# Embeddings behind each gate, rows through DRAM, norm weights inside the split, and squares summed on VectorE

## The chip, the cores and the metric

The kernel runs on one core of one Trainium2 chip. A core has five engines with a queue of instructions each: TensorE (PE; its weight loads are listed as PEld), VectorE (DVE), ScalarE (ACT), GpSimd (POOL) and SyncE (SP), which here only issues DMAs. TensorE writes its results into PSUM, eight banks of 128 partitions x 512 fp32 numbers; the other data lie in SBUF. An engine works through its queue in order, and waits on semaphores for what other engines or DMAs owe it.

The metric is the device time of one execution in microseconds (us), lower is better. Three timed executions of the kernel before gave 1090.06, 1090.41 and 1091.36; the median is 1090.41 us.

## The reference

Two layers over 256 tokens of width 2048, all in fp32, batch 1. Cut to what matters here:

```python
for i in range(2):
    hn = rmsnorm(h, e_norm[0] if i == 0 else o_norm[0])
    if i == 0:
        u = hn @ e_w_in[0]                    # q, f, i, z_a, x_b, z_b, 1024 wide each
        ya = head_rmsnorm(hgrn2(q, f, i, lbs[0]), a_norm[0]) * silu(z_a)
        yb = rg_lru(causal_conv(x_b, ...), ...) * silu(z_b)
        mix = concatenate([ya, yb]) @ e_w_out[0]
    else:
        u = hn @ o_w_in[0]                    # qk, v, og, z: 2048 each; 8 + 8 gate columns
        yc = mlstm(q, k, v, li, lf)           # running maximum of the gates as stabiliser
        yc = head_rmsnorm(yc, c_norm[0]) * sigmoid(og) * silu(z)
        mix = yc @ o_w_out[0]
    h = h + mix
    pl = rmsnorm(p[i] @ ple_w[i], ple_norm[i])      # the embedding, 256 -> 2048
    h = h + sigmoid(h @ ple_gate_w[i]) * pl
return rmsnorm(h, final_norm)
```

`rmsnorm(x, g)` is `x * rsqrt(mean(x*x) + 1e-6) * g`, along the 2048 features of a token.

## The kernel before

**Products.** Every large product is done in split precision: an fp32 operand becomes a rounded part `hi` (type fp32r) and a rest `lo = x - hi`, and hi·hi, hi·lo and lo·hi are added up in PSUM. `load_weights` (L111) has SP load 128x1024 pieces into `raw` (five buffers), ScalarE cast them into `whi` (L122) and VectorE subtract into `wlo` (L123), four buffers each. Activations are split in the same way into `ahl` tiles (`act_pair`, `split_act`; L137, L138): hi and lo side by side, 256 tokens each.

There are two forms of product. `block` (L146) has features on the partitions: 16 matmuls of 128x512 (L153, the weights' hi against hi and lo of the activations), then 16 of 128x256 (L159, the weights' lo), into one bank `mm`. `project_tok` (L179) has tokens on the partitions: two banks `mm`, one for each half of the tokens, four quarters of the inner dimension, three matmuls for each step (L194 to L196). `gate_tok` (L450) follows it with a tanh on ScalarE (L454) and a product on VectorE (L455).

**Banks.** `mm` (pool `pm`) has three PSUM banks, `mx` (pool `px`) three, `st` (pool `pst`) two.

**Side work.** What is not a large product runs beside them, as generators in named lanes (`start`, L63). `pump` (L74), called once in each `block` and once in each quarter of `project_tok`, lets each lane go on to its next `yield`; its instructions are queued behind the last large matmul, cast and split. `drain` (L81) runs a lane to its end. The order of the instructions on an engine is otherwise set by a planner with estimated costs; casts and splits of weights are put forward (`high_priority`).

**Norms.** The norm weight is applied to the activations before they are split (`gained`, L273: two scalings on VectorE, L277, then `split_act`); the factor of the token is applied behind the product. `add_square` (L265) squares on ScalarE and adds on the engine that it is given: POOL for x in the first layer (L406; VectorE for the last two of eight), for the embeddings and for h. `folded` adds the halves on POOL. `rs_tok` (L216) sums over the partitions with small matmuls (L221) and takes the inverse root on VectorE: a column `rt`, one number per token on its partition. Where a row over the tokens is needed on every partition (`rs`), `free_copy` (L259) makes it with `to_free` (L228): a diagonal matrix `dg` on VectorE and an fp32 matmul with ones (L234), copied by ScalarE. Three calls: the two layers' norms (`finish_norm`, L415; tile `hrs`), the first layer's embedding (`ple_norm`, L322; tile `plrs`).

**Layer 0.** i projection for two halves (`i_proj`, L629; the first one loads x as it goes), f and q, then the lanes `att` (HGRN2, two head groups; read out at L638) and `rg` (RG-LRU) beside the projections of x_b and the gates z_a, z_b. `out_proj` (L345) with `eo`, then the gate of the embedding (`ple_gate`, L357).

**Layer 1.** v, the gate columns, q and k, then og and z by `gate_tok`. The lane `mix` holds `gate_stats` (L829) and for each of four pairs of heads `mix(j)` (L865). `gate_stats` ends in `Mx`, the running maximum, 8 heads x 256 tokens; `split8` splits it and `spread` (L246) puts the rows of two heads on all partitions of an `mx` bank by four matmuls (L250, L251); `wt` is the constant minus these rows (L872, L873).

Behind the z gates come the features: `feature_major` (L427, lane `fm`) transposes a gate's output `u` (L438) and splits it with the norm weight into `y` (L446 on ScalarE, L447 on VectorE). The second embedding is `embed(g)` (L956), four parts of twelve matmuls (L964 to L966) into two `mm` banks, copied by VectorE (L968), squared by ScalarE (L970). The loop at L974 to L988 runs gate 0, gate 1, embed 0, gate 2, embed 1, gate 3, embed 2, a pump, embed 3, and drains `fm`. Then the rows of `ple_norm[1]` are loaded by POOL and multiplied into the parts on POOL (L993), the second row `fnr` is loaded, the sums of squares `pss` become `rp` (L999 to L1004), and `out_proj` runs with `oo` on `y`.

## Time and profile before

| | us |
|---|---|
| median of three timed executions | 1090.41 |
| the profiled execution | 1090.81 |
| its span, first to last instruction | 1089.0 |

DMA moves 200.31 MB, 184 GB/s over the span; SyncE's queue takes 53.0% of the 16 DMA engines' time, GpSimd's 1.2%.

How the lines are read. A line of the waits, "PE mm L194 <- DVE u L455: 1.9, 3, 1.2", says that TensorE's instructions of line 194, which write `mm`, stood for `u` of VectorE's line 455: 1.9 us in all, three times, 1.2 the longest. A line of the chain has the start in us, the length in us, and what ran; "x16" merges sixteen instructions. A line of the timeline has start and length in us, engine, line, operation, the tiles written and read and their shapes; in brackets stands the idle time before it and what ended it. A line of groups has "xcount | busy us in all, mean ns of one | idle us before". Matmuls overlap: a wide one is listed with 0.39 us but starts 0.23 after the one before. A line of windows has the stretch, then for PE, PEld, DVE, ACT and POOL the busy us and, in brackets, the instructions, then the granted clock, the share of DMA and GB/s.

### The profile page before, as it was taken

The page shows a single profiled execution, that of the slowest core. Times are in us where ns is not written, and L with a number is a line of the kernel's source. Part 1 is how long each engine was busy: PE and PEld are TensorE (multiplying, and loading weights), DVE is VectorE, ACT ScalarE, POOL GpSimd, SP SyncE. Part 2 cuts the span into 40 slices and gives each one's busy share as a digit, 9 for nine tenths or more (in the row PEclk, how much of TensorE's full clock was granted, in tenths as well). Part 3 has the DMA queues.
Part 4 walks back from the last instruction along what each step waited for, and adds up shares of the span by engine and source line. Part 5 has one row for each costly group of instructions (what it writes and reads, how often), then busy time and mean ns, then how long its engine had stood idle before and what let it go on. Part 6 is the DMA issues. An engine that isn't in the chain of part 4 may idle for free.

```text
span 1089.0 us, 16844 instructions
## 1 busy us (share of the span) xinstructions
PE 1064.6 (98%) x6522; PEld 913.0 (84%) x6522; DVE 753.4 (69%) x1121; ACT 580.8 (53%) x850; POOL 86.5 (8%) x74
## 2 busy tenths in 40 slices
PE   7999999999999999999999999999999999999996
PEld 6788888887888888888888888888888878888886
DVE  7968978877767556877544877764456686655565
ACT  6565455688654435555444656644445554434543
POOL 2142200000000000112000000000000120000111
PEclk9999999999999999999999999999999999999998
DMA  8655544446755555555554544445555665555552
GB/s 322 204 193 193 176 161 140 148 136 194 236 198 186 192 192 192 187 186 184 190 193 166 180 156 157 163 168 194 196 190 199 217 202 177 183 189 175 192 174 78
DMA packets 55952, 200.31 MB, mean 184 GB/s; under 512 B 6208, under 2 KB 6592, under 8 KB 55872
## 3 DMA queue, kind: packets, MB, share of 16 engines
q1 hardware_dynamic: 54720, 195.04, 53.0%
q0 software_dynamic: 1152, 4.19, 1.2%
q8 instruction: 51, 0.84, 0.3%
q14 instruction: 29, 0.24, 0.1%
HBM read 197.11 MB, written 2.10 MB: 183 GB/s over the span
## 4 chain that ended last, share of the span: by engine, by line
PE 89%; DVE 5%; ACT 4%; issue 1%; DMA 1%; SPq 0%; DVEq 0%; ACTq 0%
PE mm L153 31%; PE mm L159 17%; PE mm L194 12%; PE mm L196 12%; PE mm L195 12%; DVE wlo L123 2%; ACT whi L122 1%; PE mm L1058 1%; PE mm L1056 1%; PE mm L1057 1%; DMA raw<-in_pw_dram 1%; PE nu L897 1%; PE mx L556 1%; DVE ahl L138 0%; ACT L695 0%
## 5 line engine op out<-in xcount | busy, mean ns | idle before, releaser
L123 DVE TENSOR_TENSOR wlo<-raw,whi 128x1024 fp32r<-128x1024 f32 (+1 forms) x361 | 450.7, 1273 | 244.8 <-ACT whi L122 136.1
L122 ACT CAST whi<-raw 128x1024 fp32r<-128x1024 f32 (+1 forms) x361 | 377.1, 1047 | 331.8 <-PE mm L153 171.8
L153 PE MATMUL mm<-ahl,whi 128*128 128x512 f32 x1536 | 367.7, 392 | 2.7 <-DVE ahl L447 1.9
L153 PEld LDWEIGHTS mm<-ahl,whi 128*128 128x128 f32 x1536 | 282.3, 188 | 59.1 <-DVE ahl L447 3.0
L194 PE MATMUL mm<-whi,ahl 128*128 128x512 f32 x608 | 239.8, 394 | 2.4 <-DVE u L455 1.9
L196 PE MATMUL mm<-whi,ahl 128*128 128x512 f32 x608 | 237.1, 390 | 1.8 <-DVE ahl L138 1.8
L195 PE MATMUL mm<-wlo,ahl 128*128 128x512 f32 x608 | 237.2, 390 | 0.8 <-DVE wlo L123 0.8
L159 PE MATMUL mm<-ahl,wlo 128*128 128x256 f32 x1536 | 202.4, 285 | 0.0
L159 PEld LDWEIGHTS mm<-ahl,wlo 128*128 128x128 f32 x1536 | 195.4, 191 | 6.2
L194 PEld LDWEIGHTS mm<-whi,ahl 128*128 128x128 f32 x608 | 114.3, 188 | 27.6 <-DVE u L455 3.1
L196 PEld LDWEIGHTS mm<-whi,ahl 128*128 128x128 f32 x608 | 114.2, 188 | 27.0 <-DVE ahl L138 3.1
L195 PEld LDWEIGHTS mm<-wlo,ahl 128*128 128x128 f32 x608 | 114.3, 188 | 23.9 <-DVE wlo L123 1.1
L165 ACT COPY sm<-mm 128x256 f32<-128x256 f32 x64 | 23.7, 371 | 45.0 <-PE mm L159 45.0
L271 POOL TENSOR_TENSOR acc<-acc,sq 128x512 f32<-128x512 f32 x11 | 19.9, 1812 | 212.6 <-ACT sq L270 212.4
L166 DVE TENSOR_TENSOR mg<-mm,sm 128x256 f32<-128x256 f32 x64 | 26.7, 418 | 0.0
L782 DVE SCALAR_TENSOR_TENSOR qk<-mg,prm,qk 128x255 f32<-128x255 f32 (+2 forms) x48 | 21.3, 479 | 6.8 <-ACT qk L779 6.5
L949 POOL DMA_DIRECT2D row<-in_rows_dram x4 | 2.2, 553 | 279.8 <-DVE u L981 268.1
L1044 POOL TENSOR_TENSOR pl<-pl,row 128x512 f32<-128x512 f32 x6 | 9.2, 1533 | 153.7 <-ACT sq L1028 153.7
L446 ACT ACTIVATE ahl<-mx,prm 128x256 fp32r<-128x256 f32 x24 | 10.9, 473 | 14.6 <-PE mx L438 8.3
L1056 PE MATMUL mm<-whi,ahl 128*128 128x256 f32 x64 | 18.3, 286 | 0.0
L138 DVE TENSOR_TENSOR ahl<-hq,ahl 128x512 fp32r<-128x512 f32 x16 | 10.7, 690 | 10.8 <-ACT ahl L137 10.8
L1057 PE MATMUL mm<-wlo,ahl 128*128 128x256 f32 x64 | 18.1, 283 | 0.0
(299 smaller groups left out, 822.8 us busy)
## 6 DMA issues: line engine op xcount, KB each, us to landing
raw<-in_ew_dram SPq DMA_DIRECT2D x64, 512.0 KB, 4.8
raw<-in_g_dram SPq DMA_DIRECT2D x56, 512.0 KB, 4.3
raw<-in_eo_dram SPq DMA_DIRECT2D x32, 512.0 KB, 4.6
raw<-in_ov_dram SPq DMA_DIRECT2D x32, 512.0 KB, 4.1
raw<-in_oqk_dram SPq DMA_DIRECT2D x32, 512.0 KB, 4.5
raw<-in_oog_dram SPq DMA_DIRECT2D x32, 512.0 KB, 4.2
raw<-in_oz_dram SPq DMA_DIRECT2D x32, 512.0 KB, 4.1
raw<-in_oo_dram SPq DMA_DIRECT2D x32, 512.0 KB, 4.6
```

The source lines that it names most:

```text
L122: last["act"] = s.copy(h, r).ins
L123: last["dve"] = v.tensor_tensor(out=l, in0=r, in1=h.bitcast(F32), op=ALU.subtract).ins
L153: last["pe"] = te.matmul(ps, parts[k // 8][0][:, c:c + P], act[k // 2][2][:, (k % 2) * 512:(k % 2 + 1) * 512], start=(k == 0), stop=False).ins
L159: last["pe"] = te.matmul(ps[:, T:2 * T], parts[k // 8][1][:, c:c + P], act[k // 2][0][:, k % 2], start=False, stop=(k == KT - 1)).ins
L165: s.copy(small, ps[:, T:2 * T])
L166: v.tensor_tensor(out=dst, in0=ps[:, 0:T], in1=small, op=ALU.add)
L194: te.matmul(ps[hf], xh, wh, start=(k == 0), stop=False)
L195: te.matmul(ps[hf], xh, wl, start=False, stop=False)
L196: last["pe"] = te.matmul(ps[hf], xl, wh, start=False, stop=(k == KT - 1)).ins
L782: v.scalar_tensor_tensor(dst[:, sh:T], pi[:, 0:T - sh], pc("ccw", k * 16 + b), dst[:, sh:T], op0=ALU.mult, op1=ALU.add)
L1056: te.matmul(ps[hf], xh, wh, start=(k == 0), stop=False)
L1057: te.matmul(ps[hf], xh, wl, start=False, stop=False)
```

## The change

- `to_free`, `split8`, the old `spread` and the constant `identr` go. `free_copy` writes the column `rt` (256 single numbers) to a DRAM tile with a DMA of POOL, and reads it back on all partitions with a second one.
- `Mx` is written to DRAM by POOL in `gate_stats`. `spread(j)` is now a DMA of POOL that reads two heads' rows on all partitions into an SBUF tile `spr` (two buffers); those of pairs 0 and 1 are issued at the start of `mix(0)`, which gets one more `yield`, those of 2 and 3 from `mix(0)` and `mix(1)`.
- `gained` has ScalarE scale and cast in one instruction and VectorE multiply and subtract in one, two halves each; the tile between goes.
- All squares of x are added on VectorE.
- In the attention, the third product (`Ac`) takes an `st` bank; the product of the read out (L660) goes from POOL to VectorE; the `memset` of A comes later.
- `embed(j)` runs behind gate j, on `st` banks; it loads its part of the row of `ple_norm[1]` with POOL and multiplies it in where it copied before. POOL's products (L993) go.
- Behind the last embedding three pumps are run. The first block of `out_proj` with `oo` takes its matmuls in the order hi of 12 steps, then what is left of `fm`, lo of the 12, hi of the last 4, lo of the last 4. The sums `pss` and the load of `fnr` go into a lane `en` beside the blocks that follow.

```diff
@@ -54,6 +54,7 @@
     pm = ctx.enter_context(tc.tile_pool(name="pm", bufs=3, space=PSUM))
     pst = ctx.enter_context(tc.tile_pool(name="pst", bufs=2, space=PSUM))
+    dr = ctx.enter_context(tc.tile_pool(name="dr", bufs=2, space=bass.MemoryType.DRAM))
 
 
 
@@ -143,21 +144,34 @@
         te.matmul(o, whi, x[1][:, k], start=False, stop=False)
         last["pe"] = te.matmul(o, wlo, x[0][:, k], start=False, stop=end).ins
 
-    def block(w, act):
-
+    def block(w, act, mid=None):
 
         ps = pm.tile([P, 512], F32, name="mm", tag="mm")
         parts = load_weights(w)
-        for k in range(KT):
-            c = (k % 8) * P
-            last["pe"] = te.matmul(ps, parts[k // 8][0][:, c:c + P],
-                                   act[k // 2][2][:, (k % 2) * 512:(k % 2 + 1) * 512],
-                                   start=(k == 0), stop=False).ins
-        pump()
-        for k in range(KT):
-            c = (k % 8) * P
-            last["pe"] = te.matmul(ps[:, T:2 * T], parts[k // 8][1][:, c:c + P], act[k // 2][0][:, k % 2],
-                                   start=False, stop=(k == KT - 1)).ins
+
+        def his(ks):
+            for k in ks:
+                c = (k % 8) * P
+                last["pe"] = te.matmul(ps, parts[k // 8][0][:, c:c + P],
+                                       act[k // 2][2][:, (k % 2) * 512:(k % 2 + 1) * 512],
+                                       start=(k == 0), stop=False).ins
+
+        def los(ks):
+            for k in ks:
+                c = (k % 8) * P
+                last["pe"] = te.matmul(ps[:, T:2 * T], parts[k // 8][1][:, c:c + P], act[k // 2][0][:, k % 2],
+                                       start=False, stop=(k == KT - 1)).ins
+
+        if mid is None:
+            his(range(KT))
+            pump()
+            los(range(KT))
+        else:
+            his(range(12))
+            mid()
+            los(range(12))
+            his(range(12, KT))
+            los(range(12, KT))
         return ps
 
     def merge(dst, ps):
@@ -225,31 +239,6 @@
             v.tensor_scalar(y[:, hf:hf + 1], st[hf][:, 0:1], 1.0 / D, EPS, op0=ALU.mult, op1=ALU.add)
         return rsqrt_cols(y)
 
-    def to_free(rt):
...
-    def split8(x, name):
...
-    def spread(o, parts, h):
...
     def folded(acc, *more):
         gp.tensor_tensor(out=acc[:, 0:T], in0=acc[:, 0:T], in1=acc[:, T:2 * T], op=ALU.add)
         for x in more:
@@ -257,9 +246,10 @@
         return acc[:, 0:T]
 
     def free_copy(rt, name):
-        ps = to_free(rt)
+        d = dr.tile([T], F32, name=name + "d", tag="rsd")
+        gp.dma_start(out=d.rearrange("(h p) -> p h", h=2), in_=rt)
         rs = tp.tile([P, T], F32, name=name, tag="rsb")
-        s.copy(rs, ps)
+        gp.dma_start(out=rs, in_=d.partition_broadcast(P))
         return rs
 
     def add_square(eng, acc, src, first):
@@ -271,11 +261,12 @@
             eng.tensor_tensor(out=acc, in0=acc, in1=sq, op=ALU.add)
 
     def gained(src, g, j):
-        n = tp.tile([P, 512], F32, name="hn", tag="hn", bufs=3)
+        hi, lo, both = act_pair()
         for i in range(2):
-            k = 2 * j + i
-            v.tensor_scalar(n[:, i * T:(i + 1) * T], src[:, i * T:(i + 1) * T], pc(g, k), None, op0=ALU.mult)
-        return split_act(n, "g")
+            w, x = pc(g, 2 * j + i), src[:, i * T:(i + 1) * T]
+            s.activation(hi[:, i], x, AF.Copy, scale=w)
+            v.scalar_tensor_tensor(lo[:, i], x, w, hi[:, i].bitcast(F32), op0=ALU.mult, op1=ALU.subtract)
+        return hi, lo, both
 
     def gate_split(w, pair, act, rs, src, single):
         hi, lo, both = act_pair()
@@ -342,12 +333,12 @@
             if j % 2:
                 yield
 
-    def out_proj(hq, w, y):
+    def out_proj(hq, w, y, mid=None):
 
         act = []
         for j in range(8):
             for i in range(2):
-                ps = block(w[2 * j + i], y)
+                ps = block(w[2 * j + i], y, mid if i == j == 0 else None)
                 hh = pair_of(hq, j)[:, i * T:(i + 1) * T]
                 v.tensor_tensor(out=hh, in0=ps[:, 0:T], in1=hh, op=ALU.add)
                 v.tensor_tensor(out=hh, in0=ps[:, T:2 * T], in1=hh, op=ALU.add)
...
@@ -403,7 +393,7 @@
         xq.append(t)
         for j in (2 * i, 2 * i + 1):
             acth.append(gained(pair_of(xq, j), "en", j))
-            add_square(gp if j < 6 else v, acc, pair_of(xq, j), j == 0)
+            add_square(v, acc, pair_of(xq, j), j == 0)
         if i == 3:
             start("norm", finish_norm([folded(acc)], 0))
 
...
@@ -531,7 +520,6 @@
         res = {}
 
         A = m0.tile([P, 8, P], F32, name="A", tag="A", bufs=1)
-        gp.memset(A, 0.0)
 
         def attention(g):
 
@@ -540,6 +528,8 @@
             C = m0.tile([P, 8, 32], F32, name="C", tag="C", bufs=1)
             qf = m0.tile([P, 1024], F32, name="qf", tag="qf", bufs=1)
             v.tensor_tensor(out=qf, in0=q, in1=f, op=ALU.mult)
+            if g == 0:
+                gp.memset(A, 0.0)
             yield
             tot = f
             for B in LEVELS:
@@ -614,7 +604,7 @@
                                           (1, k4[:, c, 1], 3, q64[:, c]), (0, k64[:, c], 3, q64[:, c])):
                         te.matmul(p3[32 * x:32 * x + 32, i, 32 * y_:32 * y_ + 32], kk, qq, start=True, stop=True)
                 banks.append(p3)
-            ps = px.tile([P, 512], F32, name="mx", tag="mx")
+            ps = pst.tile([P, 512], F32, name="st", tag="st")
             for c in range(4):
                 cc = slice(c * P, (c + 1) * P)
                 te.matmul(ps[:, cc], kx[:, cc], qx[:, cc], start=True, stop=True)
@@ -657,7 +647,7 @@
                 rc = r[:, hf * 4:(hf + 1) * 4]
                 v.tensor_scalar(rc, rc, norm["rth"][:, hf:hf + 1], None, op0=ALU.mult)
             o8 = o.rearrange("p h (c e) -> p (h c) e", c=4)
-            gp.tensor_tensor(out=o8, in0=o8, in1=r.unsqueeze(2).to_broadcast([P, 8, P]), op=ALU.mult)
+            v.tensor_tensor(out=o8, in0=o8, in1=r.unsqueeze(2).to_broadcast([P, 8, P]), op=ALU.mult)
             res["o", g] = o
 
         def xb_proj(r):
@@ -844,7 +834,9 @@
             v.tensor_tensor_scan(Mx, ones[0:8, :], av, 0.0, op0=ALU.mult, op1=ALU.max)
             v.tensor_tensor(out=enm, in0=Bc, in1=Mx, op=ALU.add)
             s.activation(enm, enm, AF.Exp, scale=-1.0)
-            pM.append(split8(Mx, "Mx"))
+            d = dr.tile([8, T], F32, name="Mxd", tag="Mxd")
+            gp.dma_start(out=d, in_=Mx)
+            pM.append(d)
             yield
             yield
             yield
@@ -862,12 +854,20 @@
 
         den, ss, fac = (m1.tile([P, 16], F32, name=n, bufs=1) for n in ("den", "ss", "fac"))
 
+        spr = {}
+
+        def spread(j):
+            t = m1.tile([P, 2, T], F32, name="spr", tag="spr", bufs=2)
+            gp.dma_start(out=t, in_=pM[0][2 * j:2 * j + 2].partition_broadcast(P))
+            spr[j] = t
+
         def mix(j):
 
-            ps = px.tile([P, 512], F32, name="mx", tag="mx")
-            for i in range(2):
-                spread(ps[:, i * T:(i + 1) * T], pM[0], 2 * j + i)
-            p3 = ps.rearrange("p (i t) -> p i t", i=2)
+            if j == 0:
+                spread(0)
+                spread(1)
+                yield
+            p3 = spr[j]
             wt = m1.tile([P, 2, 384], F32, name="wt", tag="wt", bufs=1)
             v.tensor_tensor(out=wt[:, :, 0:T], in0=tri2.unsqueeze(1).to_broadcast([P, 2, T]), in1=p3, op=ALU.subtract)
             v.tensor_tensor(out=wt[:, :, T:384], in0=tri2[:, 0:P].unsqueeze(1).to_broadcast([P, 2, P]),
@@ -876,6 +876,8 @@
                 hd = 2 * j + i
                 s.activation(wt[:, i, 0:T], wt[:, i, 0:T], AF.Exp, bias=aT[:, hd:hd + 1])
                 s.activation(wt[:, i, T:384], wt[:, i, T:384], AF.Exp, bias=aT[:, 8 + hd:9 + hd])
+            if j < 2:
+                spread(j + 2)
             yield
             yield
             scw = m1.tile([P, 2, 384], F32, name="scw", tag="scw", bufs=2)
@@ -954,10 +956,12 @@
         pss = m1.tile([P, 4, 2], F32, name="pss", bufs=1)
 
         def embed(g):
+            pnr = m1.tile([P, 512], F32, name="pnr", tag="spr", bufs=2)
+            gp.dma_start(out=pnr, in_=a["rows"][0, g * 512:(g + 1) * 512].partition_broadcast(P))
             hi, lo = load_weights(a["pw1"][g // 2], halves=(g % 2,))[0]
             halves = []
             for hf in range(2):
-                ps = pm.tile([P, 512], F32, name="mm", tag="mm")
+                ps = pst.tile([P, 512], F32, name="st", tag="st")
                 for k in range(2):
                     xh, xl = (x[:, k, hf * P:(hf + 1) * P] for x in pact[0:2])
                     wh, wl = (x[:, k * 512:(k + 1) * 512] for x in (hi, lo))
@@ -965,7 +969,7 @@
                     te.matmul(ps, xh, wl, start=False, stop=False)
                     last["pe"] = te.matmul(ps, xl, wh, start=False, stop=(k == 1)).ins
                 pl = m1.tile([P, 512], F32, name="pl", tag="qk", bufs=8)
-                v.tensor_copy(pl, ps)
+                v.tensor_tensor(out=pl, in0=ps, in1=pnr, op=ALU.mult)
                 sq = tp.tile([P, 512], F32, name="sq", tag="sq")
                 s.activation(sq, ps, AF.Square, accum_out=pss[:, g, hf:hf + 1])
                 halves.append(pl)
@@ -981,17 +985,11 @@
                     v.scalar_tensor_tensor(u[:, hf, e], u[:, hf, e], fac[:, c:c + 1], nums[j][:, hf, e],
                                            op0=ALU.mult, op1=ALU.mult)
             start("fm", feature_major(u, "cn", 4 * j, y))
-            if j in (1, 2):
-                embed(j - 1)
-        embed(2)
+            embed(j)
         pump()
-        embed(3)
-        drain("fm")
-        pnr = row(0)
-        for g in range(4):
-            for pl in pls[g]:
-                gp.tensor_tensor(out=pl, in0=pl, in1=pnr[g // 2][:, (g % 2) * 512:(g % 2 + 1) * 512], op=ALU.mult)
-        fnr = row(1)
+        pump()
+        pump()
+        rows = []
 
         def total(x, n):
 
@@ -1001,9 +999,18 @@
             return x[:, 0]
 
         rp = m1.tile([P, 2], F32, name="rp", bufs=1)
-        v.tensor_scalar(rp, rsqrt_cols(total(pss, 4)), 0.5, None, op0=ALU.mult)
-
-        act = out_proj(hq, a["oo"], y)
+
+        def embed_norm():
+            yield
+            yield
+            rows.extend(row(1))
+            v.tensor_scalar(rp, rsqrt_cols(total(pss, 4)), 0.5, None, op0=ALU.mult)
+            yield
+
+        start("en", embed_norm())
+        act = out_proj(hq, a["oo"], y, lambda: drain("fm"))
+        drain("en")
+        fnr = rows
 
 
         hss = m1.tile([P, 5, 2], F32, name="hss", bufs=1)
```

More of the change, by code (lines that the diff above doesn't have):

```diff
@@ L226, in rs_tok @@
         return rsqrt_cols(y)
-    def to_free(rt):
-        dg = tp.tile([P, T], F32, name="dg", tag="dg", bufs=1)
-        v.tensor_tensor(out=dg.rearrange("p (h t) -> p h t", h=2), in0=ident.unsqueeze(1).to_broadcast([P, 2, P]),
-                        in1=rt.unsqueeze(2).to_broadcast([P, 2, P]), op=ALU.mult)
-        st = pst.tile([P, 512], F32, name="st", tag="st")
-        te.matmul(st[:, 0:T], ones[:, 0:P], dg, start=True, stop=True)
-        return st[:, 0:T]
-    def split8(x, name):
-        n = x.shape[0]
-        hi = tp.tile([8, T], F32R, name=name + "h", tag="s8h", bufs=1)[0:n, :]
-        lo = tp.tile([8, T], F32R, name=name + "l", tag="s8l", bufs=1)[0:n, :]
-        v.tensor_copy(hi, x)
-        v.tensor_tensor(out=lo, in0=x, in1=hi.bitcast(F32), op=ALU.subtract)
-        return hi, lo
-    def spread(o, parts, h):
-        n = parts[0].shape[0]
-        w = identr[0:n, h:h + 1].to_broadcast([n, P])
-        te.matmul(o, w, parts[0], start=True, stop=False)
-        te.matmul(o, w, parts[1], start=False, stop=True)
     def folded(acc, *more):
@@ L461, in derive @@
         sy.dma_start(out=cst, in_=a["cst"])
-        v.tensor_copy(identr, ident[0:8, 0:8])
         yield
```

1 line of the change is left out of this document (removed).

## The prediction

> **What bounds the kernel now.** I read the page's head first, to see which engine the span belongs to.
>
> ```profile
> span 1089.0 us, 16844 instructions
> PE 1064.6 (98%) x6522; PEld 913.0 (84%) x6522; DVE 753.4 (69%) x1121; ACT 580.8 (53%) x850; POOL 86.5 (8%) x74
> PEclk9999999999999999999999999999999999999998
> PE 89%; DVE 5%; ACT 4%; issue 1%; DMA 1%; SPq 0%; DVEq 0%; ACTq 0%
> ```
>
> TensorE is busy 98% of the span at a clock that is never held back, and 89% of the chain that ended last is its own. So an edit earns time in two ways only: it takes matmuls off TensorE, or it takes away a wait of TensorE. The view of waits, TensorE alone (total us, times, longest), gives the second kind:
>
> ```profile
> PE mm L142 <- ACT whi L122: 6.6, 2, 5.0
> PE mm L194 <- DVE u L455: 1.9, 3, 1.2
> PE mm L153 <- DVE ahl L447: 1.9, 2, 1.7
> PE mm L196 <- DVE ahl L138: 1.8, 2, 1.1
> PE mm L153 <- ACT sq L970: 0.8, 1, 0.8
> ```
>
> The first row is the wait for the first weights, which nothing here touches. The other four are 6.4 us and stand at places that the change edits, or next to one (Part 5). With what leaves TensorE, that is the size of the case: some 10 us of 1090.
>
> **Part 1: matmuls that leave TensorE.** The view of the chain, merged, shows the blocks of `block`: 16 wide matmuls (L153), 16 narrow ones (L159).
>
> ```profile
> 90.62 3.65 PE mm L153 x16
> ...
> 96.19 3.66 PE mm L153 x16
> ...
> 102.20 3.65 PE mm L153 x16
> ...
> 618.58 3.65 PE mm L153 x16
> ...
> 624.99 3.65 PE mm L153 x16
> ```
>
> ```profile
> L234 PE MATMUL st<-dg,ones 128*128 128x256 f32 x6 | 1.9, 397 | 0.0
> L250 PE MATMUL mx<-Mxh,identr 8*128 8x256 f32 x8 | 2.4, 325 | 0.0
> ```
>
> An undisturbed block steps 96.19 - 90.62 = 5.57 us (so one wide matmul takes 0.228, the narrow sixteen 1.92). The block at 96.19, in which `to_free` (L234) sits, steps 6.01: 0.44 us. Six records at two a call are three calls: 3 x 0.44 = 1.3. The block at 618.58, with the four small matmuls of `spread`, steps 6.41: 0.84 us; eight L250 at two a pair are four pairs: 4 x 0.84 = 3.4. All of it is time of the bounding engine. Sum of the part: **-4.7**.
>
> What takes their place are POOL's DMAs, hidden if they land in time:
>
> ```profile
> row<-in_rows_dram POOLq DMA_DIRECT2D x4, 512.0 KB, 6.0
> 84.41 0.68 DVE L176 TENSOR_TENSOR mg<-mg,hrs 128x512 f32<-128x512 f32 x1
> 607.69 0.67 DVE L844 TENSOR_TENSOR_SCAN Mx<-ones,li 8x256 f32<-8x256 f32 x1
> 622.92 0.69 DVE L872 TENSOR_TENSOR wt<-cst,mx 128x512 f32<-128x512 f32 x1
> ```
>
> A POOL load takes 6.0 us to land, so a write and a read behind it take some 12. `Mx` is done at 608.4, `wt` read it at 622.9, and the added yield puts `wt` one block later, about 628.5: 14 to 20 us for the first pair, a whole period of four blocks more for the others. The first `hrs` is read at 84.4, and its column `rt` stands before 47.6 (the ScalarE row of Part 2): 37 us. The layer-1 norm and `plrs` feed nothing sooner. The trace shows no write of 256 single elements to DRAM, as `hrs` now needs: from below its cost to TensorE is 0 however fast it lands, from above it is what the slower rival works out. I take the 6.0 of POOL's only row for it, and 6.0 for the read. So 0. POOL's queue is in order: the read waits for the write there, and behind both stand only POOL's own multiplies of `pl`, which are needed 300 us later.
>
> **Part 2: the start.** One window (busy of PE, PEld, DVE, ACT, POOL), then single instructions by time:
>
> ```profile
> 14.00:31.00 17.00, 15.17 (x90) 12.69 (x89) 17.00 (x24) 12.16 (x18) 10.09 (x5) 1.00 0.84 316
> 16.50 0.68 DVE L138 TENSOR_TENSOR ahl<-hn,ahl 128x512 fp32r<-128x512 f32 x1
> 18.75 3.53 POOL L271 TENSOR_TENSOR acc<-acc,sq 128x512 f32<-128x512 f32 x2 [2.92 <-ACT sq L270]
> 21.05 1.77 DVE L138 TENSOR_TENSOR ahl<-hn,ahl 128x512 fp32r<-128x512 f32 x1
> L277 DVE TENSOR_SCALAR hn<-xq,prm 128x256 f32<-128x256 f32 x16 | 6.9, 468 | 0.0
> L981 DVE SCALAR_TENSOR_TENSOR u<-u,fac,num 128x256 f32<-128x256 f32 x16 | 7.3, 481 | 0.2
> 47.59 0.69 ACT L635 ACTIVATE vt<-mm,rcr 128x512 f32<-128x512 f32 x1 [2.40 <-DVE rcr L208]
> ```
>
> VectorE is busy 17.00 of 17 us and TensorE waits for its `ahl`. The same subtraction takes 0.68 us at 16.50 and 1.77 at 21.05, while POOL adds squares: the adds cost VectorE more than their place.
>
> Per pair of tiles VectorE did two L277 and one L138; it will do two products with subtraction at 0.48 (L981). Over eight pairs: 6.9 + 7.6 (six at 0.68, two stretched to 1.77) before, 16 x 0.48 = 7.7 after, and five adds of L138's size at 0.68 = 3.4 arrive: 14.5 becomes 11.1. VectorE is over 3 us ahead, and the chain to `ahl` loses one change of engines. ScalarE gets two half-width scalings for one cast, on an engine busy 12 of 17. So the 1.8 us go. But `vt` at 47.59 waits for the norm column and frees the bank that the next projection needs; it must come earlier by as much. It hangs on VectorE, which is ahead: **-1.8**, bounds 0 and -2.4. The `memset` of A only moves on POOL; layer 1's `gained` stands where no wait is listed: 0.
>
> **Part 3: banks of the embeddings.**
>
> ```profile
> 838.33 0.39 PE L966 MATMUL mm<-whi,ahl 128*128 128x512 f32 x1
> 839.05 0.50 PE L194 MATMUL mm<-whi,ahl 128*128 128x512 f32 x1 [0.33 <-DVE u L455]
> ```
>
> An embedding takes two of the three `mm` banks, so the next gate waits for `u` to release one: 0.72 instead of 0.23, 0.49 lost, and again behind the next gate. With the `st` banks, empty at that time, both go: **-1.0**.
>
> **Part 4: from the last gate to the output projection.**
>
> ```profile
> 878.94 0.87 PE mx L438 x8
> ...
> 887.78 0.24 PE mm L196
> ...
> 907.96 1.91 PE mm L159 x16
> ```
>
> ```profile
> 891.91 2.32 DVE L123 TENSOR_TENSOR wlo<-raw,whi 128x1024 fp32r<-128x1024 f32 x1
> 894.55 1.87 DVE L968 COPY pl<-mm 128x512 f32<-128x512 f32 x3
> 897.60 2.47 DVE L999 TENSOR_TENSOR pss<-pss 128x2 f32<-128x2 f32 x2
> 902.02 0.87 DVE L447 SCALAR_TENSOR_TENSOR ahl<-mx,prm,ahl 128x256 fp32r<-128x256 f32 x2
> ```
>
> From 888.02 to 907.96 TensorE had 24 embedding matmuls (24 x 0.228 = 5.5), eight transposes (0.87), two runs of L153 (7.3) and one of L159 (1.9): 15.6 us of work in 19.9, so 4.3 lost. VectorE's queue says why: a split slowed by POOL's row multiplies, three copies, then `pss` waiting for ScalarE, all ahead of the `ahl` that the block's last matmuls need. After the change one embedding is left there, the copy does the row's multiply (so POOL's L993 goes), `pss` is summed later, and the block has 12 wide and 12 narrow matmuls that need no late `ahl`. Cover from the gate's end: 12 x 0.228 + 12 x 0.228 + 0.87 + 12 x 0.12 = 7.8 us. The way to `ahl`: the tanh and the product that make `u`, both 128x512, at L138's 0.68; two L981, 1.0; transposes 0.9; four scalings and a last subtraction at L447's 0.44, 2.2: 5.5 alone, 9.1 with three weight operations ahead at L123's 1.2 or so (row in Part 5). So from nothing to 1.3 us stay late, and 2.5 with a fourth; I take 0.8: **-3.5**.
>
> **Part 5: work that moves onto VectorE where it sets the pace.**
>
> ```profile
> 240.00:260.00 20.00, 18.10 (x78) 14.16 (x76) 13.01 (x14) 16.58 (x27) 0.00 (x0) 1.00 0.43 139
> 237.07 4.09 DVE L718 SCALAR_TENSOR_TENSOR xc<-mg,prm,xc 128x255 f32<-128x255 f32 x6
> 237.31 2.00 POOL L660 TENSOR_TENSOR o<-o,hnr 128x1024 f32<-128x1024 f32 x1 [57.46 <-ACT av L688]
> L123 DVE TENSOR_TENSOR wlo<-raw,whi 128x1024 fp32r<-128x1024 f32 (+1 forms) x361 | 450.7, 1273 | 244.8 <-ACT whi L122 136.1
> ```
>
> Here TensorE idles some 2 us with ScalarE busiest, behind a chain through L718. L660 on VectorE has L123's size, 1.3, and the six L718, stretched beside POOL to 4.09, fall to L981's 6 x 0.48 = 2.9: 1.2 back. I take 0, with +1.3 and, if the idle goes whole, -2 as bounds; the extra bank that attention leaves to the gates of the recurrence points down.
>
> **Sum.** -4.7 - 1.8 - 1.0 - 3.5 = -11.0. The profiled execution took 1090.8 (its span and 1.8 around it), the median is 1090.4: 1079.8 or 1079.4. I say **1079.6**.
>
> **Rivals.**
> - The start hands its gain on: `rt` isn't earlier, and the next projection waits for `vt` by 1.8. For it: `vt` started right at `rcr`. Against it: VectorE's lead. Time 1081.4.
> - The cover of Part 4 fails: planned casts and splits go ahead of `ahl`, and 2.7 us stay late, 1.9 more than taken. For it: exactly that stood there before. Time 1081.5; with the first, 1083.3.
> - Part 5 unties: the bank and a lighter queue shorten the chain into 260, and the idle 2 us go: 1077.6.
> - It doesn't do what it says: the planner, which orders every engine anew, opens other waits as large as those closed. For it: VectorE has stretches without slack; against it: 4.7 us leave TensorE whatever the order. Time 1090.
> - **Slower:** the scattered write of `rt`, 256 elements, is slow, and VectorE stands at the first `mg` times `hrs` (L176) for it, with the weight splits (L123) that TensorE lives on queued behind. Free are the 37 us of Part 1 and 5.6 more, since four `wlo` buffers hold two blocks; each us beyond is lost. It undoes the gain from 37 + 5.6 + 11 = 53.6 us on, that is where, beside the read's 6.0, each element takes (53.6 - 6.0) / 256 = 0.19 us one behind another; at 60 us the time is 1079.6 + 17.4 = 1097.0. For it: no row of before bounds such a write. Against it: 512 KB land in 6.0.
>
> [...]
>
> **Chances.** The sum within some 2 us: 0.50; start handed on: 0.14; cover fails: 0.14; unties: 0.10; nothing gained: 0.06; slower: 0.06. The range from 1076.0 to 1084.0 leaves out the last two and some of the tails. About 0.2% (2.2 us) is what can be told from no change: faster 0.88, same 0.06, slower 0.06.
>
> **What would show it.** Right: no L234 and L250 rows, blocks near 620 step 5.6; `ahl` subtractions at the start all near 0.5 and TensorE's wait for them gone; no wait of L194 for `u` behind embeddings; the first L153 block of `oo` without a wait over 1 us. Wrong: a row in which `wt`, `pl` or `mg` waits for a DMA; a wait of L194 for `vt` near 45; new waits in 200 to 260.

## The result and the profile after

The kernel after the change takes 1078.38 us, the median of four executions (1077.04 to 1079.74), beside 1090.53 for the kernel before (1090.06 to 1091.36, four executions). The ratio is 0.9885, with a 95% interval of 0.9873 to 0.9897. The profiled execution took 1078.11, its span is 12.7 us shorter (1089.0 to 1076.3).

The head of the page of the kernel after, with the chain by engine:

```profile
span 1076.3 us, 16798 instructions
PE 1055.6 (98%) x6500; PEld 910.4 (85%) x6500; DVE 735.1 (68%) x1106; ACT 584.8 (54%) x863; POOL 67.8 (6%) x72
PE 93%; DVE 2%; ACT 2%; issue 1%; DMA 1%; SPq 0%; DVEq 0%; ACTq 0%
```

TensorE still bounds the kernel, and more of the chain is now its own: 93% for 89%. It has 22 matmuls fewer. The view of waits, TensorE alone, is short:

```profile
PE mm L143 <- ACT whi L123: 7.4, 2, 6.1
PE mx L674 <- DVE xc L708: 2.3, 1, 2.3
PE mx L546 <- DVE qf L530: 1.9, 1, 1.9
```

The four waits that stood beside that for the first weights are gone, and so are four smaller ones (0.2 to 0.8 us) that the view before listed; two have come up, at 122 and 244 us, where none was listed before. (Lines have moved: L194 to L196 are now L208 to L210, L153 and L159 are L155 and L162, L123 is L124, L438 and L447 are L428 and L437, L660 is L650, L718 is L708, L551 is L541.)

**Where the time went.** TensorE's queue has the same points in both kernels: the first norm's sums, the third norm's, and the transposes of the gates 0 and 2 in layer 1. Their first rows in the timelines of TensorE, before:

```profile
42.12 0.50 PE L221 MATMUL st<-ones,acc 128*128 128x1 f32 x4
516.76 0.39 PE L221 MATMUL st<-ones,acc 128*128 128x1 f32 x3
826.79 0.38 PE L438 MATMUL mx<-cst,u 128*128 128x128 f32 x2
878.78 0.38 PE L438 MATMUL mx<-cst,u 128*128 128x128 f32 x2
```

and after:

```profile
39.90 0.50 PE L235 MATMUL st<-ones,acc 128*128 128x1 f32 x4
513.28 0.28 PE L235 MATMUL st<-ones,acc 128*128 128x1 f32 x2
822.18 0.38 PE L428 MATMUL mx<-cst,u 128*128 128x128 f32 x2
872.93 0.38 PE L428 MATMUL mx<-cst,u 128*128 128x128 f32 x2
```

The differences are -2.22, -3.48, -4.61 and -5.85. Two corrections are needed: after the change one embedding (twelve matmuls of 0.228, 2.74 us) stands ahead of the transposes of gate 0 that stood behind them before, and so one less is left behind those of gate 2. The table lists the terms:

| stretch | predicted | measured |
|---|---|---|
| Part 2, the start, to the first norm | -1.8 | -2.2 |
| Part 1, `to_free`, 3 x 0.44 | -1.3 | -1.3 |
| Part 1, `spread`, 4 x 0.84 | -3.4 | -3.4 |
| Part 3, banks of the embeddings | -1.0 | -1.2 |
| Part 4, last gate to `oo` | -3.5 | -4.2 |
| Part 5, and all else between 42 and 513 | 0 | -0.4 |
| sum | -11.0 | -12.7 |

Part 3 is -5.85 + 4.61. Two of the `to_free` lie between 42 and 513, where the points move by -1.26: 0.88 is theirs (taken in order, the large matmuls of the two timelines draw apart by 0.46 us at 48 and by 0.49 at 99), and -0.4 is left. The third lies with `spread` between 513 and 822: -4.61 + 3.48 - 2.74 = -3.87, which is 0.44 + 3.4. In the chain of waits of the kernel after, the block with the first pair of heads:

```profile
620.21 3.65 PE mm L155 x16
...
625.78 3.65 PE mm L155 x16
```

It steps 5.57 us, where the block with the four small matmuls stepped 6.41.

The first row of the table is the least certain. The kernel after and nine of the experiments have the same start, and in their traces the first norm's sums begin between 38.89 and 40.67 us, so that from single traces this row is -1.5 to -3.2.

**The start.** One window (busy PE, PEld, DVE, ACT, POOL), the group of the subtractions between 12 and 42, and the first `vt`:

```profile
14.00:31.00 17.00, 17.00 (x104) 15.26 (x103) 16.18 (x26) 16.96 (x32) 0.00 (x0) 1.00 0.92 349
```

```profile
L268 DVE SCALAR_TENSOR_TENSOR ahl<-xq,prm,ahl 128x256 fp32r<-128x256 f32 x16 | 7.4, 475 | 0.2 <-ACT ahl L267 0.2
```

```profile
43.25 0.69 ACT L625 ACTIVATE vt<-mm,rcr 128x512 f32<-128x512 f32 x1 [0.27 <-DVE rcr L222]
```

TensorE is busy 17.00 of 17 us, where it was 15.17: these 1.8 us are the two waits for `ahl`. GpSimd adds nothing beside it, and no subtraction is stretched: sixteen at 0.475 on the mean. `vt` came 47.59 - 43.25 = 4.3 us earlier, so nothing was handed on.

**The end of layer 1.** From the chain of waits, the transposes of gate 2 and the narrow matmuls of the second `oo` block:

```profile
873.09 0.87 PE mx L428 x8
...
895.15 1.91 PE mm L162 x16
```

Before, the same two points were 907.96 - 878.94 = 29.02 apart, now 22.06; less the one embedding that is 4.2. No wait for `ahl` is listed.

**The two new waits.** The timeline of GpSimd, the second round trip:

```profile
92.88 0.74 POOL L250 DMA_DIRECT2D plrsd<-rcr  x1 [15.53 <-DVE rcr L222]
...
107.44 13.28 POOL L332 TENSOR_TENSOR pl<-pl,plrs 128x512 f32<-128x512 f32 x8 [5.88 <-DMA plrs<-plrsd]
```

The row comes back 14.6 us after its write was issued, and GpSimd's eight products with it run to 120.7. Before, they began at 101.33 and were over before the operation that TensorE needs next. The same group, and that operation, before:

```profile
101.33 14.81 POOL L341 TENSOR_TENSOR pl<-pl,plrs 128x512 f32<-128x512 f32 x8 [22.48 <-ACT plrs L262]
121.50 1.22 DVE L542 TENSOR_TENSOR qf<-q,f 128x1024 f32<-128x1024 f32 x1
```

and after, with what TensorE does:

```profile
119.63 2.18 DVE L530 TENSOR_TENSOR qf<-q,f 128x1024 f32<-128x1024 f32 x1
121.86 0.73 PE L546 MATMUL mx<-qf,k 128*32 128x16 f32 x64 [1.88 <-DVE qf L530]
```

`qf` takes 2.18 instead of 1.22 us, and TensorE stands 1.88 us for it. The second one is in VectorE's queue near 241:

```profile
236.04 1.22 DVE L650 TENSOR_TENSOR o<-o,hnr 128x1024 f32<-128x1024 f32 x1
...
238.75 2.28 DVE L696 TENSOR_TENSOR_SCAN tt<-av,it 128x1024 f32<-128x1024 f32 x1
240.95 2.33 DVE L124 TENSOR_TENSOR wlo<-raw,whi 128x1024 fp32r<-128x1024 f32 x2
243.20 0.47 DVE L708 SCALAR_TENSOR_TENSOR xc<-mg,prm,xc 128x253 f32<-128x253 f32 x1
```

The product of the read out (L650) is here now, and the last of six L708 stands behind a scan and two splits. TensorE waits 2.3 us for it; in return the waits near 255 are gone. Taken in order, the large matmuls of the two timelines give the exchange: 2.0 us lost at 122, 1.0 won near 215 (the bank of the third product), 2.6 lost at 244, 3.2 won from 255 to 260.

### The profile page after: what moved, and what is told of

It is laid out like the page before. It is cut to its first block, busy times and chain, and to the rows that moved or that the text cites. A ratio compares the mean times of both kernels' runs of the same rounds, so it can differ in the third digit from the quotient of the medians.

```text
span 1076.3 us, 16798 instructions
## 1 busy us (share of the span) xinstructions
PE 1055.6 (98%) x6500; PEld 910.4 (85%) x6500; DVE 735.1 (68%) x1106; ACT 584.8 (54%) x863; POOL 67.8 (6%) x72
## 4 chain that ended last, share of the span: by engine, by line
PE 93%; DVE 2%; ACT 2%; issue 1%; DMA 1%; SPq 0%; DVEq 0%; ACTq 0%
PE mm L155 31%; PE mm L162 16%; PE mm L208 12%; PE mm L209 12%; PE mm L210 12%; DVE wlo L124 1%; PE mm L1065 1%; PE mm L1064 1%; PE mm L1063 1%; PE nu L899 1%; PE mx L546 1%; DMA raw<-in_pw_dram 1%; PE mx L428 0%; ACT whi L123 0%; PE mm L143 0%
## 5 line engine op out<-in xcount | busy, mean ns | idle before, releaser
L124 DVE TENSOR_TENSOR wlo<-raw,whi 128x1024 fp32r<-128x1024 f32 (+1 forms) x361 | 444.9, 1255 | 257.9 <-ACT whi L123 145.7
L123 ACT CAST whi<-raw 128x1024 fp32r<-128x1024 f32 (+1 forms) x361 | 377.5, 1048 | 333.9 <-PE mm L155 163.4
L155 PE MATMUL mm<-ahl,whi 128*128 128x512 f32 x1536 | 367.8, 391 | 0.0
L155 PEld LDWEIGHTS mm<-ahl,whi 128*128 128x128 f32 x1536 | 282.0, 188 | 55.7 <-DVE ahl L139 0.6
L208 PE MATMUL mm<-whi,ahl 128*128 128x512 f32 x608 | 238.7, 393 | 0.0
L210 PE MATMUL mm<-whi,ahl 128*128 128x512 f32 x608 | 236.7, 389 | 0.0
L162 PE MATMUL mm<-ahl,wlo 128*128 128x256 f32 x1536 | 201.8, 284 | 0.0
L162 PEld LDWEIGHTS mm<-ahl,wlo 128*128 128x128 f32 x1536 | 195.7, 191 | 6.2
L210 PEld LDWEIGHTS mm<-whi,ahl 128*128 128x128 f32 x608 | 114.1, 188 | 24.0
L208 PEld LDWEIGHTS mm<-whi,ahl 128*128 128x128 f32 x608 | 114.2, 188 | 23.3
L261 POOL TENSOR_TENSOR acc<-acc,sq 128x512 f32<-128x512 f32 x6 | 9.7, 1621 | 193.8 <-ACT sq L260 193.8
L1063 PE MATMUL mm<-whi,ahl 128*128 128x256 f32 x64 | 18.3, 285 | 0.0
L1065 PE MATMUL mm<-whi,ahl 128*128 128x256 f32 x64 | 18.1, 283 | 0.0
L190 DVE TENSOR_TENSOR mg<-mg,hrs 128x512 f32<-128x512 f32 (+1 forms) x25 | 17.8, 714 | 0.3
L143 PE MATMUL mm<-ahl,whi 128*128 128x256 f32 x32 | 10.0, 314 | 7.4 <-ACT whi L123 7.4
```

The costliest lines, as they stand in the source:

```text
L123: last["act"] = s.copy(h, r).ins
L124: last["dve"] = v.tensor_tensor(out=l, in0=r, in1=h.bitcast(F32), op=ALU.subtract).ins
L155: last["pe"] = te.matmul(ps, parts[k // 8][0][:, c:c + P], act[k // 2][2][:, (k % 2) * 512:(k % 2 + 1) * 512], start=(k == 0), stop=False).ins
L162: last["pe"] = te.matmul(ps[:, T:2 * T], parts[k // 8][1][:, c:c + P], act[k // 2][0][:, k % 2], start=False, stop=(k == KT - 1)).ins
L208: te.matmul(ps[hf], xh, wh, start=(k == 0), stop=False)
L210: last["pe"] = te.matmul(ps[hf], xl, wh, start=False, stop=(k == KT - 1)).ins
```

## The experiments

Each one is the kernel after with one edit (two, or three, where it says so). Times are the median and the extremes of four executions; the ratio is to the kernel before on the same chip.

### The row for GpSimd's products, made by TensorE again

```diff
-        rs = free_copy(rt, "plrs")
+        rs = free_copy_pe(rt, "plrs")   # diagonal, L234's matmul, copy by ScalarE, as before
```

> The kernel after, with the row plrs alone made by the matmul with ones again, as before the change. Theory: the new wait of 1.9 us of TensorE for qf at 120 us is GpSimd's eight products of pl, which now start some 9 us later, behind a round trip through DRAM of 14.6 us, and stretch qf from 1.2 to 2.2 us. With the matmul they start near 98, the wait goes, and the matmul costs 0.44: 1.4 us faster than the kernel after, 1077.0. Rival: the wait comes from the new order on VectorE; then it stays, and the time is 0.4 longer, 1078.8.

1076.38 us (1075.5 to 1076.84), ratio 0.9869 (0.9854 to 0.9884). The waits of TensorE:

```profile
PE mm L143 <- ACT whi L123: 6.1, 2, 5.1
PE mx L684 <- DVE xc L718: 2.3, 1, 2.3
```

The wait for `qf` is gone. 1.9 us of wait away and one `to_free` of 0.44 back on TensorE make -1.5; the profiled executions differ by 1.7, the medians by 2.0. So the wait at 120 comes from the round trip through DRAM. In the kernels whose edits lie elsewhere TensorE waits at this place for `qf`, or for the `q` and `k` beside it, by 0.8 to 1.9 us; only here and in the later version with the same edit is nothing listed. The stretched `qf` is not the whole of it: in one kernel below (plain block and sums first) GpSimd's products are over at 119.62, `qf` takes 1.22 from 119.94 on, and TensorE still waits 0.9 for it. This version has the lowest median of all, 14 us under the kernel before.

### Squares of x on GpSimd again

```diff
-            add_square(v, acc, pair_of(xq, j), j == 0)
+            add_square(gp if j < 6 else v, acc, pair_of(xq, j), j == 0)
```

> The kernel after, with the squares of x added on GpSimd again for the first six pairs; the split with the norm weight stays. Theory: the adds on GpSimd were what held VectorE's splits at the start, so TensorE's waits for ahl near 20 to 30 us come back, with single VectorE instructions there stretched to over 1 us; 1 to 2.2 us slower than the kernel after (1079.4 to 1080.6 us). Rival: the shorter way from x to ahl removed the waits; then no wait comes back and the time stays within 0.5 us.

1082.23 us (1080.69 to 1083.13), ratio 0.9922 (0.9907 to 0.9937): 3.9 us slower than the kernel after. From the waits of TensorE, then the timelines of VectorE and GpSimd:

```profile
PE mm L209 <- DVE wlo L124: 1.8, 2, 1.0
...
PE mm L208 <- ACT vt L625: 1.0, 1, 1.0
```

```profile
24.70 2.95 DVE L268 SCALAR_TENSOR_TENSOR ahl<-xq,prm,ahl 128x256 fp32r<-128x256 f32 x2
```

```profile
24.27 3.10 POOL L261 TENSOR_TENSOR acc<-acc,sq 128x512 f32<-128x512 f32 x2 [1.90 <-ACT sq L260]
```

Beside GpSimd's adds two subtractions take 2.95 us, 1.5 each where they take 0.475 alone. The splits of weights queued behind them come late (TensorE waits for `wlo`, at 28.84 and 64.97, and not for `ahl` as the theory had it), and the norm too, so that here the start does hand its loss on: 1.0 us is a wait for `vt`, the first rival's mechanism. That makes more than the 1 to 2.2 us that were expected. About 1.6 us of the profiled execution is another matter (the last section).

### The scaling ahead of the split as before

```diff
...
-            s.activation(hi[:, i], x, AF.Copy, scale=w)
-            v.scalar_tensor_tensor(lo[:, i], x, w, hi[:, i].bitcast(F32), op0=ALU.mult, op1=ALU.subtract)
...
+            v.tensor_scalar(n[:, i * T:(i + 1) * T], src[:, i * T:(i + 1) * T], pc(g, k), None, op0=ALU.mult)
+        return split_act(n, "g")
```

> The kernel after, with the two scalings, cast and subtraction of before in place of the scaling within cast and split, both layers; the squares stay on VectorE. Theory: with GpSimd quiet at the start VectorE's load there rises from 16 x 0.48 to 16 x 0.30 + 8 x 0.68 = 10.2 us, 2.5 us more; TensorE waits at the start by 0 to 1 us, time 1078.4 to 1079.4. Rival: the shorter way did it; then the two waits of some 2 us come back whole, 1080.4.

1078.61 us (1077.63 to 1080.08), ratio 0.9892 (0.9877 to 0.9906): no difference from the kernel after. The one wait of TensorE at the start:

```profile
PE mm L209 <- DVE wlo L124: 0.4, 1, 0.4
```

So the start is won by the squares on VectorE alone. The merged scaling takes work off VectorE, 7.4 us for the 10.3 of the old form here (5.0 of scalings, 5.3 of subtractions between 12 and 42), but with GpSimd silent there is enough room for the old form.

### The product of the read out on GpSimd again

```diff
-            v.tensor_tensor(out=o8, in0=o8, in1=r.unsqueeze(2).to_broadcast([P, 8, P]), op=ALU.mult)
+            gp.tensor_tensor(out=o8, in0=o8, in1=r.unsqueeze(2).to_broadcast([P, 8, P]), op=ALU.mult)
```

> The kernel after, with the product of the read out on GpSimd again. Theory: that product on VectorE is why the wait behind the gates of the recurrence at 255 to 260 us (3 us before) went, and why a new one of 2.3 us for xc at 241 came: the same lateness met elsewhere. Undone, the wait at 241 goes and the one near 255 comes back: -2.3 + 3.0, 0 to 1 us slower, 1078.4 to 1079.4. Rival: the PSUM bank that attention leaves free removed the wait at 255; then both are gone, 2.3 us faster, 1076.1.

1079.61 us (1079.55 to 1081.86), ratio 0.9899 (0.9883 to 0.9916): 1.2 us slower by the medians. From the waits of TensorE:

```profile
PE mm L208 <- ACT whi L123: 1.2, 1, 1.2
PE mm L209 <- DVE wlo L124: 0.8, 1, 0.8
PE mm L208 <- DVE u L445: 0.7, 1, 0.7
```

The wait at 241 is gone and the old ones near 255 are back, 2.7 for 2.3. Part 5 is such an exchange: the move neither wins nor loses more than about 1 us.

### The third product of the attention in an `mx` bank again

```diff
-            ps = pst.tile([P, 512], F32, name="st", tag="st")
+            ps = px.tile([P, 512], F32, name="mx", tag="mx")
```

> The kernel after, with the third product of the attention in an mx bank again. Theory: TensorE's 1 us loss at 214 us comes back, but TensorE waits at 241 for VectorE's xc in any case, so that wait gets shorter by as much: 0, 1078.4. Rival: the bank is worth its 1 us in full: 1079.4.

1077.35 us (1077.19 to 1077.59), ratio 0.9876 (0.9861 to 0.989). From the waits:

```profile
PE mx L674 <- DVE xc L708: 1.2, 1, 1.2
PE mx L674 <- ACT A L614: 0.5, 1, 0.5
```

TensorE waits 0.5 us for `A` at 212, and 1.1 less for `xc` at 241. The `st` bank is worth nothing in the sum: what comes earlier there waits longer at the next place.

### The factor of the read out in a later product

The first experiment's edit, and besides the factor `r` of the read out is not multiplied into `o` at all, but into the later product with `u`:

```diff
-                    v.tensor_tensor(out=u[:, hf], in0=u[:, hf], in1=res["o", g][:, hf], op=ALU.mult)
+                    for c in range(4):
...
+                        v.scalar_tensor_tensor(u[:, hf, e], u[:, hf, e], r[:, hf * 4 + c:hf * 4 + c + 1], o[:, hf, e],
+                                               op0=ALU.mult, op1=ALU.mult)
```

> A version made from the findings: the kernel after, with plrs made by the matmul with ones, and the read out's product left out as an instruction of its own: its factor is applied where the gate is multiplied in (eight products of 128x128 with a column in place of two of 128x512). Theory: VectorE has xc done ahead of the splits, so the wait of 2.3 us at 241 goes, and with it the half clock that followed in some runs; 1076.4 - 2.3 = 1074.1, in a narrow spread. Rival: ScalarE is late there too and the wait near 255 comes back, as in a6_o_pool; then 1076 to 1077.5.

1076.98 us (1076.0 to 1077.37), ratio 0.9874 (0.986 to 0.9889). From the waits (in this kernel and in the first experiment lines stand ten further down):

```profile
PE mm L208 <- DVE u L455: 1.3, 1, 1.3
PE mm L209 <- DVE wlo L124: 0.8, 1, 0.8
```

The wait at 241 is gone without the product, and the one near 255 is back although GpSimd is all but idle there (busy 0.2 us from 250 to 260). By the ratio it isn't better than the first experiment: between 235 and 260 the waits make 1.2 to 2.7 us in each of the orders tried, at one place or the other.

### Rows of the running maximum by TensorE again

`spread` with its four small matmuls a pair, `split8` and `identr` as before.

```diff
-            p3 = spr[j]
+            ps = px.tile([P, 512], F32, name="mx", tag="mx")
+            for i in range(2):
...
+                te.matmul(ps[:, i * T:(i + 1) * T], w, pM[0][0], start=True, stop=False)
+                te.matmul(ps[:, i * T:(i + 1) * T], w, pM[0][1], start=False, stop=True)
```

> The kernel after, with the rows of Mx spread by matmuls again (split in two parts, four matmuls a pair of heads), and the added yield kept. Theory: 16 matmuls at 0.84 us per four come back on TensorE, 3.4 us slower, 1081.8. Rival: the round trip also cost something somewhere that the trace does not show as a wait; then less than 3, or the round trip's replacement took a wait away too, and it is more than 4.

1083.71 us (1081.24 to 1084.04), ratio 0.9932 (0.9918 to 0.9947): 5.3 us slower by the medians. From the chain of waits:

```profile
622.83 3.65 PE mm L155 x16
...
629.24 3.65 PE mm L155 x16
```

The block steps 6.41 again. From the third norm to the transposes of gate 0 TensorE needs 312.3 us (515.90 to 828.22 in its timeline) for 308.9 in the kernel after: 3.4, the term of Part 1. In the profiled executions another 2.6 lie ahead of 515.9 (513.28 in the kernel after), where this edit changes nothing but a small constant; the clock (last section) was half for two stretches there, from 122.7 and from 245.6, at some 1.6 us each.

### Embeddings in `mm` banks again

```diff
-                ps = pst.tile([P, 512], F32, name="st", tag="st")
+                ps = pm.tile([P, 512], F32, name="mm", tag="mm")
```

> The kernel after, with the embeddings in mm banks again. Theory: TensorE waits for u behind three embeddings by 0.5 each: 1.0 to 1.5 slower, 1079.4 to 1079.9. Rival: behind each gate the bank is free in time anyway: 1078.4.

1081.16 us (1078.61 to 1081.45), ratio 0.9905 (0.989 to 0.992). From the waits:

```profile
PE mm L208 <- DVE u L445: 0.9, 3, 0.3
```

The wait for `u` is back, three times, 0.3 us listed. What each costs is seen in TensorE's timeline: from the transposes of gate 0 to those of gate 1, and from there to gate 2, it takes 26.00 us, as in the kernel before, for 25.38 and 25.37 in the kernel after; from the third norm to gate 0 it takes 0.62 more too. So an embedding in `mm` banks loses 0.62, the three 1.9, and the two of Part 3 the 1.2 that were measured. The profiled execution is 3.0 slower than that of the kernel after; 0.4 more is lost behind the last embedding (next section), and the rest lies ahead of the third norm, where the clock behind the wait at 241 cost about 1.6 and the start was 0.7 earlier.

### The end of layer 1, taken apart

First, `fm` drained ahead of an ordinary first block:

```diff
-        act = out_proj(hq, a["oo"], y, lambda: drain("fm"))
+        drain("fm")
+        act = out_proj(hq, a["oo"], y)
```

> The kernel after, but the first block of oo takes its matmuls in the plain order (16 wide, then 16 narrow) and the rest of fm is drained ahead of it; embeddings, sums and rows stay as changed. Theory: the way to the last ahl is 5.5 us alone and up to 9 with weight work ahead, the cover without the narrow matmuls in between is 6.3 instead of 7.8, so TensorE waits for ahl by 0 to 2.8 us; 0.5 to 1.5 slower, 1079 to 1080. Rival: the new order of the block is nearly all of the gain there; then some 3.5 to 4 us come back, 1082.

Second, the sums `pss` ahead of the projection instead of in the lane `en`:

```diff
         start("en", embed_norm())
+        drain("en")
         act = out_proj(hq, a["oo"], y, lambda: drain("fm"))
-        drain("en")
```

> The kernel after, but the sums pss, rp and the load of the second row are issued ahead of the projection oo again, not in a lane beside it. Theory: the small sums wait on VectorE for ScalarE's squares, ahead of the last ahl, as before; of the 4 us won there some 1 comes back, 1079.4. Rival: the order of the block covers it; 1078.4, no wait of TensorE for ahl.

Third, both together:

> The kernel after with two edits behind the last gate undone at once: plain order of the first block of oo, and the sums pss with the load of the second row ahead of it. Each alone cost nothing. Theory: they cover for one another, and with both undone the sums stand ahead of the last ahl and nothing hides it: TensorE waits for ahl by 0.5 to 1.5 us, 1079 to 1080. Rival: neither matters once GpSimd's products and one embedding are gone from there; no wait, 1078.

Fourth, both, and the embeddings at their old places:

```diff
-            embed(j)
+            if j in (1, 2):
+                embed(j - 1)
+        embed(2)
         pump()
+        embed(3)
...
```

> As c1_plain_and_pss, and the embeddings stand where they stood before (two behind the last gate), in st banks and with the row multiplied in as they are copied. What is left of the change behind the last gate is that GpSimd's eight products are gone. Theory: the second embedding's two copies and squares stand ahead of ahl on VectorE and ScalarE; 1.5 to 3 us of the 4.2 come back, 1080 to 1081.5. Rival: GpSimd's products, which stretched the splits there, were the cause; then under 0.5 comes back, 1078 to 1078.5.

| | median us | ratio to before, 95% |
|---|---|---|
| plain block | 1077.91 (1077.88 to 1080.19) | 0.9888 (0.9871 to 0.9904) |
| sums first | 1077.75 (1077.48 to 1079.01) | 0.9881 (0.9867 to 0.9896) |
| both | 1079.21 (1079.06 to 1080.3) | 0.9899 (0.9882 to 0.9915) |
| both, embeddings late | 1080.45 (1078.79 to 1082.36) | 0.9908 (0.9893 to 0.9923) |

None of the four shows a wait of TensorE for `ahl`. The third and the fourth took about as long as their theories said, but by luck: those theories had waits and losses here, and there are next to none. The last one, from the chain of waits: the transposes of gate 2, and the narrow matmuls of the second `oo` block.

```profile
870.77 0.87 PE mx L428 x8
...
895.85 1.90 PE mm L162 x16
```

25.08 us, with one embedding (2.74) more than in the kernel after: 22.34 for 22.06. With the order of the block, the lane of the sums and the place of the embeddings all undone, 0.3 of the 4.2 us come back. What is left of the change there is that GpSimd's eight row products are gone and that the embeddings use `st` banks (and two more pumps, behind which `fm` is drained anyway). So about 3.9 of the 4.2 us belong to these two together. How they share it is open, since no run puts the products back. One figure bears on it: with the embeddings in `mm` banks and all else kept, this stretch took 898.20 - 875.76 = 22.44, 0.4 more than in the kernel after. If nothing else covers for the banks there, the missing products are the larger share; that VectorE was slower beside GpSimd's work is shown at the start (1.5 us for 0.475) and at `qf` (2.18 for 1.22).

The longer medians of the last two lines don't come from this end. From the transposes of gate 2 to the end of the span the first three take 203.3 to 203.5 us, for 203.4 in the kernel after. What differs beyond that lies ahead of the third norm, where these edits change nothing, and where all four profiled executions have the half clock behind the wait at 241.

## Why the prediction was right

**Part 1** was right in size: the steps of the blocks are those of an undisturbed block, and the rows of `Mx` land in time. It was wrong that the round trips cost TensorE nothing. From the DMA groups of the kernel after (KB each, median us to landing):

```profile
hrs<-hrsd POOLq DMA_DIRECT2D x2, 128.0 KB, 6.9
...
hrsd<-rcr POOLq DMA_DIRECT2D x2, 1.0 KB, 9.4
```

The write of 256 single numbers lands in 9.4 us, and with the read it makes 16 for the 12 that was taken, far inside the slack of 37; no row shows VectorE waiting for it, so the slower rival is out. What made the write slow, its 256 elements or what ran beside it, no run separates. The cost came elsewhere: "behind both stand only POOL's own multiplies of `pl`, which are needed 300 us later" is true of their result, not of their place. Moved by 6.1 us, they lay on VectorE's `qf` and what stands ahead of it, and the 1.9 us wait followed. The first experiment shows it.

**Part 2** was right; the 0.4 beyond it is less than what the same start varies by. The reason given first, GpSimd's adds stretching VectorE, is shown by the second experiment (1.5 us for 0.475); the reason given second, 14.5 us of VectorE's work falling to 11.1 with the merged scaling, isn't needed: the third experiment puts the old scaling back and loses nothing. The first rival (gain handed on through `vt`) didn't happen, but its mechanism is there: with the squares on GpSimd the wait for `vt` is 1.0 us.

**Part 3** was right, 1.2 for 1.0, and undoing it gives the same 0.62 for each embedding.

**Part 4** had the right sign, and its reason was in the wrong place. The cover that was worked out (twelve wide and twelve narrow matmuls that need no late `ahl`) can be taken away at no cost, the later sums too. The step "the copy does the row's multiply (so POOL's L993 goes)", or the `st` banks that Part 3 priced by their own waits alone, carries nearly all of the 4.2. The 0.8 us taken as staying late didn't stay. That the size came out within 0.7 us is luck in part, since the sum was made of a cover that wasn't needed.

**Part 5** was right at 0 within the bounds, by an exchange that the prediction named as a danger, new waits in 200 to 260: 2.3 us at 241 for what was lost near 255.

So Part 1 came out as taken and the others 0.2 to 0.7 us better. The wait at 120 is paid for within the last term: without its 1.9 us that term would stand at -2.3. The one cost that wasn't priced and cautions that weren't needed went against each other, and that the total is off by only 1.2 us is luck to that extent. One reading was too strong, though no term rests on it: the clock row taken as "never held back" ends in an 8, and the trace has the clock at half from 1082.3 us to the end, where TensorE has nothing left to do.

## What to carry to other kernels

The work of an engine off the critical path wasn't free here: beside GpSimd's products VectorE's `qf` took 2.18 us for 1.22, and TensorE waited 1.9 us there. Before such work is moved in time, look at what VectorE does in the stretch where it will land, not only at when its result is needed. Where one queue bounds a stretch, taking a piece from one place (a bank, a product) may only move the wait to the next, so sum the waits over the stretch. Where the clock falls behind a wait, as it did here in eight traces of ten behind one of 2.3 us, set a stretch of one trace beside the same stretch of another: behind the third norm these traces agree to 0.2 us where the edit changes nothing, and ahead of it they differ by 1.5 with the same code (512.72 to 514.27 at the third norm). And undo the parts of a change one at a time: here the most elaborate one, the order of the first block, could go without loss.

## What the hardware did unexpectedly

**TensorE's clock was half behind a wait of 2.3 us.** The experiment with the plain block, in windows of 3.41 us, the granted clock ahead of the last two columns:

```profile
239.97:243.38 3.41, 1.44 (x7) 1.25 (x7) 1.92 (x3) 3.36 (x6) 0.00 (x0) 1.00 0.46 168
243.40:246.80 3.40, 3.40 (x10) 2.64 (x9) 0.42 (x1) 2.52 (x4) 0.00 (x0) 0.50 0.43 140
246.82:250.23 3.41, 3.41 (x17) 2.81 (x16) 2.48 (x3) 2.76 (x4) 0.00 (x0) 1.00 0.44 127
```

The wait for `xc` (2.3 us) ends at 241.9. From 243.4 the clock is half for one window, ten matmuls for seventeen in the next, about 1.6 us lost. The kernel after had the same wait without it:

```profile
243.22:246.62 3.40, 2.89 (x13) 2.45 (x14) 0.45 (x2) 3.36 (x5) 0.00 (x0) 1.00 0.71 247
```

In the experiment with the product on GpSimd, behind waits of 1.2 and 0.8 us close together, the windows show 0.50 for two such stretches, from 256.8 to 263.6; its profiled execution, with a granted clock of 0.995 over the span, is the longest of its four (0.997 and 0.998 in the others).

Ten of the traces have the wait of 2.3 us. The stretch follows in eight, and neither in the kernel after nor in the first experiment. What differs is where the wait falls. Counted from the first moment at full clock (10.5 us in the kernel before, 11.1 in the kernel after), each stretch starts at a whole multiple of 3.413 us, with the plain block at the 68th; the half clock behind TensorE's last work starts on the same grid, 1071.79 us after that moment in the kernel before and 1058.13 in the kernel after, the 314th and the 310th. The 14 traces can be cut into windows of this grid. Of the windows at full clock between 100 and 1060 us, eight have TensorE busy 32 to 43%, and each is followed by half clock. Over the whole of the traces five have 46 to 49%, and two of these are followed by it; of those with 50% or more none is. In the two traces without the stretch a border of the grid lies inside the wait, which so falls into two windows: at 241.41 in the first experiment, with 51% ahead of it, and at 243.21 in the kernel after, with 1.62 of 3.41 us, 47 to 48%:

```profile
239.80:243.21 3.41, 1.62 (x8) 1.05 (x6) 3.41 (x4) 2.13 (x5) 0.00 (x0) 1.00 0.04 10
```

So by these traces it depends on its place in the grid whether a wait of 2.3 us costs 1.6 more. That the executions of one kernel differ by this is likely but not shown, since only one of each has a trace, and the clock over the whole span doesn't tell: it is 0.997 in the profiled execution of the kernel after, without the stretch, and 0.997 in that with the embeddings late, which has it.

**VectorE was slower beside GpSimd.** `qf` took 2.18 us beside GpSimd's products and 1.22 alone, the subtraction at the start 1.5 beside its adds and 0.475 alone.

**A write of 256 single elements landed late.** The writes of `rt`, 1 KB each, took 9.4 us by the median of two for `hrs` and 7.8 for `plrs`; 8 KB of `Mx`, in the same queue, 4.1:

```profile
Mxd<-Mx POOLq DMA_DIRECT2D x1, 8.0 KB, 4.1
```
